# FFN down with twelve folded pairs and weight sums made ahead, in place of eight pairs with sums made on the spot

## The chip, the core and the metric

The kernel runs on one core of one Trainium2 chip. Its time is device microseconds. The profiled times below come from one execution of the kernel before; the time of the runs is the median of three.

## The reference

One layer over 256 latent tokens of width 2048, with 256 context tokens that only feed the attention. All is float32. Cut to what the change touches:

```python
mod = jax.nn.silu(c) @ w_mod[l] + b_mod[l]          # 6 * 2048 columns
...
y = (sigmoid(ga) * (oa @ w_br_a) + sigmoid(gb) * (ob @ w_br_b)) @ w_o
x = x + gt1 * rms_norm(y, g_attn_post[l])
h = modulate(rms_norm(x, g_ffn_pre[l]), sh2, sc2)
# conv_ffn: w_up is 2048 x 11264, w_down is 5632 x 2048
u = depthwise_conv(h @ w_up, conv_w, conv_b)        # three taps along the tokens
a, g = jnp.split(u, 2, axis=-1)
x = x + gt2 * rms_norm((silu(g) * a) @ w_down, g_ffn_post[l])
```

## The kernel before

**Products.** TensorE makes a float32 product out of three: both operands are split into a high part `hi` of type fp32r and a rest `lo`, and hi x hi, lo x hi and hi x lo are summed in PSUM (`product`, L1377). `split` (L140) makes the two parts of a tile: ACT copies the source into `hi` with rounding (L144), then DVE subtracts `hi` from the source (L148). So ACT's half always comes before DVE's half of the same tile, and a matmul can begin when the first is there.

**Weights.** `ws` holds the weights from the value projection to FFN down as blocks of 128 x 2048 floats (1 MB), in the order of use. `raw_block` (L130) loads one from SP's queue into a ring of four buffers (`raw`), which the tiles of the modulation (`wm_b`) go through too. `block` (L205) hands out the next block: it splits the one after it (`split_to`) and issues loads up to `ahead` blocks further (`load_to`); `halves` (L151) makes the `wh` and `wl` of a plain block in two halves of 1024 columns, in two sets of buffers. A raw buffer is free for its next load when both parts are made, or, for a modulation tile, when its product is done. SP issues its loads in the order of its list, so a load that waits for a buffer holds up those behind it.

**Modulation.** 64 of the columns of `mod` are made by DVE, one per tile of `wm_b`: `mods` (L237) multiplies the tile with the row of silu(c) (`crb`) and sums along it (L247, 128 x 2048). Six of them go beside Wo and sixteen beside FFN up.

**Wo.** `norm_gain` (from L981) multiplies by `w_o` in four chunks `c` of 512 output columns, each of four blocks `g`; a block is four contraction tiles times two token halves times three products, 24 matmuls at L994. Beside each block, `beside(c, g)` runs: the two loads of `x`, and in the first three chunks one modulation product behind each of the blocks g = 1, 2, 3. Six tiles are left by then, so the last calls do nothing.

**FFN up.** A loop over the 44 tiles `j` of the hidden width, each with an activation block (i = 0) and a gate block (i = 1). The work on the last block's result is queued behind the split of the next weights: evacuation (ACT `half_u` L222, DVE `u` L223), the convolution's taps (ACT L1264, DVE L1265 and L1267), and `gate` (L1271: silu, product and the split of the activations). In every even `j` from 4, behind the gate block, one modulation product runs on DVE.

**FFN down.** The hidden width is 44 contraction tiles; the output is made in two halves `h` of 1024 columns, as two chunks of 512. A **direct** block D (L1383) has four contraction tiles and one chunk: 4 tiles x 2 token halves x 3 = 24 matmuls. A **folded** block S (`fold`, L1390) has one pair of contraction tiles and both chunks: it takes the 2 x 2 blocks of the activations (two token halves, two tiles) and of the weights (two tiles, two chunks), forms sums of them, and makes seven products in place of eight, 7 x 3 = 21 matmuls, by Strassen's scheme. Three products use weights as they are (`wh`, `wl`), four use sums of weights (`th`, `tl`). `folded` (L181) makes both on the spot: two splits of the plain weights (512 and 1024 wide), four additions of 512 columns in place in the raw buffer (L190), two splits of the sums (1024 wide). The sums of the activations are made in `gate` (L1291) and kept split in `fs`, seven tiles per pair. `J0, NS` say that tiles 24 to 39 are the eight pairs; `SEQ` gives the order of blocks in a half:

```python
SEQ = "DSDSDSDDSDSDDSDSDSDDDD"   # 14 D, 8 S
wts = first_wts if h == n == 0 else block(3)
```

The products' sums are put together by closures (`late`) behind the half's last S.

**What sets the order.** The program is written in one order, and a scheduler makes a list per engine from it; `issue_after` holds a piece of work behind a given instruction. The engines run their lists in order and wait on each other by semaphores; a tile's next use waits for the readers of its buffer. POOL has no work in the stages that are touched.

## Time and profile before

| | us |
|---|---|
| median of 3 runs (1495.61 to 1495.78) | 1495.72 |
| the profiled execution | 1495.41 |
| its span | 1493.6 |
| PE busy in it | 1484.2 |
| DVE busy | 1220.0 |
| ACT busy | 821.9 |
| Wo, products at L994 | 672.95 to 760 |
| FFN up | to 1256.5 |
| FFN down, products at L1379 | 1256.7 to 1485.75 |

A row of a group reads: line, engine, operation, output <- inputs, shape and type of the output <- of the input, count, then busy time and the mean ns of one, then the idle time of the engine just before them and what ended it ("<-ACT wh L144": ACT's work on `wh`). A row of the timeline or chain starts with the time from the start of the span and the duration in us, and ends in the wait before it. A row of the windows has the stretch, its length, the busy us (and instructions) of PE, PEld, DVE, ACT and POOL, the granted clock of TensorE, the busy share of the DMA engines and GB/s. A row of the DMA issues ends in the median us from issue to landing. Shares above 1.00 come from packets that overlap in the records.

### The profile page before, as it was taken

How to read it: one execution, taken by the hardware profiler on the slowest of the kernel's cores; microseconds unless marked ns; L12 is line 12 of the kernel's file. 1: busy time of each engine (PE TensorE's matmuls, PEld its weight loads, DVE VectorE, ACT ScalarE, POOL GpSimd, SP SyncE). 2: the span in 40 equal slices, each digit the busy share in tenths (PEclk: the TensorE clock that was granted, in tenths of full speed). 3: DMA queues.
4: the chain of work that ended last, by engine and by line, in shares of the span. 5: the costliest groups of instructions: out<-in, count | busy, mean ns of one | idle time of the engine just before them, and what ended most of it. 6: DMA issues, size and time to landing. Idle time of an engine off the chain costs nothing.

```text
span 1493.6 us, 21738 instructions
## 1 busy us (share of the span) xinstructions
PE 1484.2 (99%) x8491; PEld 1279.4 (86%) x8491; DVE 1220.0 (82%) x1851; ACT 821.9 (55%) x1363; POOL 1.8 (0%) x11
## 2 busy tenths in 40 slices
PE   9999999999999999999999999999999999999998
PEld 6877889998888888888888888888888888888886
DVE  4499878989988888877877887887888878887887
ACT  5553324777764455455667555555555565455443
POOL 0000000000000000000000000000000000000000
PEclk9999999999999999999999999999999999999999
DMA  9988699754467888779856666766666654655652
GB/s 371 399 317 338 250 384 348 267 190 170 143 254 294 326 319 325 292 273 357 309 207 224 247 236 224 254 232 222 251 230 232 216 196 163 231 212 185 268 216 106
DMA packets 61159, 383.72 MB, mean 257 GB/s; under 512 B 6512, under 2 KB 8960, under 8 KB 18304
## 3 DMA queue, kind: packets, MB, share of 16 engines
q1 hardware_dynamic: 60480, 381.52, 68.3%
q8 instruction: 67, 1.10, 0.3%
q10 hardware_dynamic: 576, 0.80, 0.2%
q14 instruction: 36, 0.29, 0.1%
HBM read 378.05 MB, written 4.25 MB: 256 GB/s over the span
## 4 chain that ended last, share of the span: by engine, by line
PE 97%; DMA 1%; DVE 1%; ACT 1%; issue 0%; SPq 0%; DVEq 0%
PE pu L217 21%; PE c L1379 12%; PE pu L218 11%; PE pv L760 7%; PE pg L217 7%; PE pk L498 7%; PE py_o L994 6%; PE pq L217 4%; PE pb L217 4%; PE pg L218 4%; PE x L1379 3%; PE pq L218 2%; PE pb L218 2%; PE po L902 1%; PE s L871 1%; PE pt L893 1%
## 5 line engine op out<-in xcount | busy, mean ns | idle before, releaser
L148 DVE TENSOR_TENSOR wl<-raw,wh 128x1024 fp32r<-128x1024 f32 (+1 forms) x444 | 520.8, 1201 | 119.8 <-ACT wh L144 119.0
L144 ACT ACTIVATE wh<-raw 128x1024 fp32r<-128x1024 f32 (+1 forms) x444 | 444.7, 1037 | 204.9 <-PE pg L217 54.6
L217 PE MATMUL pu<-h,wh 128*128 128x512 f32 x1404 | 487.6, 390 | 0.0
L218 PE MATMUL pu<-h,wl 128*128 128x256 f32 x1404 | 395.9, 282 | 0.0
L217 PEld LDWEIGHTS pu<-h,wh 128*128 128x128 f32 x1404 | 263.6, 188 | 55.0
L218 PEld LDWEIGHTS pu<-h,wl 128*128 128x128 f32 x1404 | 265.4, 189 | 0.0
L217 PE MATMUL pg<-h,wh 128*128 128x512 f32 x464 | 161.5, 390 | 0.0
L1379 PE MATMUL c<-wh,ff 128*128 128x512 f32 x448 | 137.9, 389 | 0.0
L218 PE MATMUL pg<-h,wl 128*128 128x256 f32 x464 | 130.8, 282 | 0.0
L247 DVE SCALAR_TENSOR_TENSOR raw<-raw,crb 128x2048 f32<-128x2048 f32 x48 | 109.7, 2285 | 11.2 <-DMA raw<-in_wm_b_dram 11.1
L498 PE MATMUL pk<-h,ku 128*128 128x512 f32 x480 | 117.4, 398 | 0.8 <-ACT h L410 0.4
L222 ACT ACTIVATE half_u<-pu 128x256 f32<-128x256 f32 x88 | 33.4, 382 | 147.8 <-PE pu L218 147.8
L217 PE MATMUL pq<-h,wh 128*128 128x512 f32 x304 | 108.8, 396 | 0.1
L498 PEld LDWEIGHTS pk<-h,ku 128*128 128x128 f32 x480 | 87.7, 188 | 24.1 <-issue 3.9
L217 PEld LDWEIGHTS pg<-h,wh 128*128 128x128 f32 x464 | 87.1, 188 | 18.2
L760 PE MATMUL pv<-wh,h 128*128 128x512 f32 (+1 forms) x384 | 101.5, 354 | 0.0
L1379 PEld LDWEIGHTS c<-wh,ff 128*128 128x128 f32 x448 | 84.0, 188 | 17.3
L217 PE MATMUL pb<-h,wh 128*128 128x512 f32 x256 | 89.4, 390 | 0.0
L218 PEld LDWEIGHTS pg<-h,wl 128*128 128x128 f32 x464 | 87.7, 189 | 0.0
L1379 PE MATMUL c<-wl,ff 128*128 128x512 f32 x224 | 87.4, 390 | 0.0
L218 PE MATMUL pq<-h,wl 128*128 128x256 f32 x304 | 85.5, 281 | 0.0
L994 PE MATMUL py_o<-wh,zz 128*128 128x512 f32 x256 | 78.3, 389 | 0.0
(258 smaller groups left out, 2091.4 us busy)
## 6 DMA issues: line engine op xcount, KB each, us to landing
raw<-in_ws_dram SPq DMA_DIRECT2D x222, 1024.0 KB, 4.9
raw<-in_wm_b_dram SPq DMA_DIRECT2D x64, 1024.0 KB, 4.9
raw<-in_wm_sc_dram SPq DMA_DIRECT2D x15, 1024.0 KB, 7.6
raw<-in_wkt_dram SPq DMA_DIRECT2D x10, 1024.0 KB, 7.7
raw<-in_wm_sh_dram SPq DMA_DIRECT2D x8, 1024.0 KB, 9.5
sd<-in_wm_sd_dram SPq DMA_DIRECT2D x6, 1024.0 KB, 6.3
raw<-in_wk_dram SPq DMA_DIRECT2D x7, 768.0 KB, 8.1
crb<-sild SPq DMA_DIRECT2D x5, 1024.0 KB, 8.9
```

Source lines behind the costliest of these rows:

```text
L144: a_ = nc.scalar.activation(hi, src, AF.Copy)
L148: v_ = nc.vector.tensor_tensor(out=lo, in0=src, in1=hi, op=ALU.subtract)
L217: nc.tensor.matmul(pt[:, :], wh[:, w], a, start=first and i == 0, stop=False, skip_group_check=True)
L218: nc.tensor.matmul(pt[:, :S], wl[:, w], a[:, 0], start=False, stop=last and i == n - 1, skip_group_check=True)
L222: a_ = nc.scalar.activation(t[:], pt[:, S:], AF.Copy)
L247: nc.vector.scalar_tensor_tensor(out=r, in0=r, scalar=1.0, in1=row, op0=ALU.mult, op1=ALU.mult, accum_out=modx[:, j : j + 1])
L498: nc.tensor.matmul(pk[:], wt[:, w], hh[:, :, k, a], start=k == 0 and a == 0 and wt is wh, stop=k == KT - 1 and a == 1)
L760: nc.tensor.matmul(pv[i][:, :nw], src[:, k, a, t0 : t0 + P], wt[:, w], start=k == 0 and q == 0, stop=k == KT - 1 and q == 2)
L871: nc.tensor.matmul(s_ps, qs[hd][:, a, qt * P : qt * P + P], k_[:, w], start=q == 0, stop=q == 2)
L893: nc.tensor.transpose(pt[:, b * P : b * P + P], sms[hd, qt][:, b * P : b * P + P], ident[:])
L994: p_ = nc.tensor.matmul(py[t][:], act[:, k, a, t * P : t * P + P], wt[:, w], start=k == 0 and q == 0, stop=k == nk - 1 and q == 2)
L1379: nc.tensor.matmul(pt[:], a(i), wt[:, w], start=k not in begun, stop=stop and q == 2, skip_group_check=True)
```

## The change

**More pairs.** Tiles 16 to 39 are twelve pairs; a half of FFN down is 10 D and 12 S, in the order DSS, six times, and four D.

**Sums of weights ahead.** There are 24 blocks S (twelve pairs in two halves), and each needs one block of sums of weights (1 MB). They are made before FFN down and kept in DRAM (`sumd`): SP loads the S block into the raw ring (`load_sum`), DVE makes the sums in place in one subtraction of 1024 columns and two operations of 512 (`sum_part`), and POOL's queue writes the 1 MB to `sumd` (`nc.gpsimd.dma_start`). Four are made beside Wo: at block i = 4c + g of Wo stands a product of the modulation (m) or a sum (T) by `WO = " mmTmTmTmTm"`. Twenty are made beside FFN up, in the even j from 4; its modulation products go to the odd j from 5. In FFN down an S block loads its `sumd` (1 MB) and the three chunks of 512 columns of the plain weights (0.75 MB). The four additions in place are gone there.

**The order inside S.** The columns of an S block in `ws` stand in the order b1, a1, a0, b0. The four products of sums come first, in two tiles `t0` and `t1` with one buffer each, and the three of plain weights after them; the splits of the next S block's sums are put between the products.

**Four pairs unsplit.** Of pairs 2, 4, 6 and 8 the activations are kept as they are (`late_a`) and are summed and split in FFN down (`late_split`), in each half, in the D block ahead of the pair, into one buffer `late_f`.

```diff
@@ -56,9 +56,13 @@
-J0, NS = 24, 8
+J0, NS = 16, 12
 ND0 = (FT - 2 * NS) // 4
-SEQ = "DSDSDSDDSDSDDSDSDSDDDD"
+SEQ = "DSSDSSDSSDSSDSSDSSDDDD"
+LATE = (2, 4, 6, 8)
+NSUM = 2 * NS
+WO = " mmTmTmTmTm"
+SUMS_UP = range(4, FT, 2)
@@ -67,6 +71,15 @@
+def kept(p):
+    return p - sum(q < p for q in LATE)
+def block_of_sum(n):
+    h, p = divmod(n, NS)
+    return B_DN + h * len(SEQ) + [i for i, kind in enumerate(SEQ) if kind == "S"][p]
@@ -171,26 +185,57 @@
+    sum_of = {b0 + block_of_sum(n): n for n in range(NSUM)}
+    wsum, folding = {}, []
     def load_to(i):
         for q in range(min(i, len(srcs) - 1) + 1):
             if q not in raws:
-                raws[q] = raw_block(*srcs[q])
-
-    def folded(r):
...
+                if q in sum_of:
+                    wsum[q] = raw_block(sumd[sum_of[q]])
+                    nraw[0] += 1
+                    r = raws[q] = wp.tile([P, 2048], F32, tag="raw", bufs=4, name=f"raw{nraw[0]}")
+                    for w in (slice(0, 512), slice(1024, 2048)):
+                        sync.dma_start(out=r[:, w], in_=srcs[q][0][:, w])
+                else:
+                    raws[q] = raw_block(*srcs[q])
+    def split_sum(q, half):
+        w = slice(half * 1024, half * 1024 + 1024)
+        t = [folding[0].tile([P, 1024], F32R, tag=f"t{half}{c}", bufs=1, name=f"t{half}{c}{q}") for c in "hl"]
+        split(t[0][:], t[1][:], wsum[q][:, w])
+        parts[q][1].append(t)
+    def folded(q):
         h, lo = (
-            wp.tile([P, 2048 + 128], F32R, tag=f"w{q}", bufs=2, name=f"w{q}{nraw[0]}")[:, :2048] for q in "hl")
+            wp.tile([P, 2048 + 128], F32R, tag=f"w{c}", bufs=2, name=f"w{c}{q}")[:, :2048] for c in "hl")
+        parts[q] = (h, lo), []
+        if SEQ[(q - b0 - B_DN - 1) % len(SEQ)] == "D":
+            with tc.issue_after(last[0]), tc.issue_after(last[1]):
+                for half in range(2):
+                    split_sum(q, half)
+        for w in (slice(0, 512), slice(1024, 2048)):
+            split(h[:, w], lo[:, w], raws[q][:, w])
+    tosum, nsum = [], [0]
+    def load_sum():
+        if nsum[0] + len(tosum) < NSUM:
+            tosum.append(raw_block(ws[block_of_sum(nsum[0] + len(tosum))]))
+    def sum_part(i):
+        if not tosum:
+            return
+        r = tosum[0]
+        q = [r[:, n * 512 : n * 512 + 512] for n in range(4)]
+        if i == 0:
+            nc.vector.tensor_tensor(out=r[:, :1024], in0=r[:, :1024], in1=r[:, 512:1536], op=ALU.subtract)
+            return
+        nc.vector.tensor_tensor(out=q[2], in0=q[0], in1=q[2], op=ALU.add)
+        nc.vector.tensor_tensor(out=q[3], in0=q[3], in1=q[2], op=ALU.subtract)
+        nc.gpsimd.dma_start(out=sumd[nsum[0]], in_=tosum.pop(0))
+        nsum[0] += 1
@@ -1049,8 +1094,16 @@
-            if c < 3 and g:
-                mods(1, crb[:], (c, g) != (2, 3))
+            i = 4 * c + g
+            if i < len(WO):
+                with tc.issue_after(last[1]):
+                    if WO[i] == "T":
+                        sum_part(0)
+                        sum_part(1)
+                    elif i:
+                        mods(1, crb[:], 0)
+                if 0 < i < len(WO) - 1:
+                    (load_sum if WO[i + 1] == "T" else load_mod)()
@@ -1249,7 +1302,9 @@
-    fs = fp.tile([P, NS, 2, 7, P], F32R, name="fs")
+    fs = fp.tile([P, NS - len(LATE), 2, 7, P], F32R, name="fs")
+    late_a = fp.tile([P, len(LATE), 2, S], F32, name="late_a")
+    late_f = fp.tile([P, 2, 7, P], F32R, name="late_f")
@@ -1270,27 +1325,35 @@
-        nc.vector.tensor_tensor(out=a[:], in0=a[:], in1=g[:], op=ALU.mult)
+        p, odd = divmod(j - J0, 2)
+        o = late_a[:, LATE.index(p), odd] if is_folded(j) and p in LATE else a[:]
+        nc.vector.tensor_tensor(out=o, in0=a[:], in1=g[:], op=ALU.mult)
         if not is_folded(j):
             d = direct_tile(j)
             split(ff[:, d, 0], ff[:, d, 1], a[:])
...
+        elif p not in LATE:
+            if odd:
+                act_sums(bank(f"st{p}"), first[0][:], a[:])
+            act_split(fs[:, kept(p)], a[:], odd)
+            if odd:
+                act_split(fs[:, kept(p)], None, 2)
             first[:] = [a]
+    def act_split(dst, a, part):
+        hi, lo = (dst[:, q].rearrange("p i t -> p (i t)") for q in range(2))
+        o, w = ((0, P), (P, 2 * P), (3 * P, 4 * P))[part]
+        split(hi[:, o : o + w], lo[:, o : o + w], total[0] if part == 2 else a[:, :w])
+    def act_sums(t, e, a):
+        e0, e1 = e[:, :P], e[:, P:]
         t_ = [t[:, i * P : i * P + P] for i in range(4)]
         for o, x, y, op in (
+            (t_[2], e0, e1, ALU.subtract), (t_[0], e1, a[:, P:], ALU.add), (t_[1], t_[0], e0, ALU.subtract),
             (t_[3], a[:, :P], t_[1], ALU.subtract)):
             nc.vector.tensor_tensor(out=o, in0=x, in1=y, op=op)
-        split(hi[:, 3 * P :], lo[:, 3 * P :], t[:])
+        total[:] = [t[:]]
+    total = []
@@ -1318,7 +1381,12 @@
-                mods(i if j % 2 == 0 and j > 3 else 0, crb)
+                if j in SUMS_UP:
+                    sum_part(i)
+                elif i and j > 4:
+                    mods(1, crb, 0)
+                if i:
+                    (load_sum if j + 1 in SUMS_UP else load_mod if j > 3 else list)()
@@ -1387,18 +1455,30 @@
-        def fold(wts, p):
-            (wh, wl), (th, tl) = wts
+        def fold(wts, p, behind=None):
+            (wh, wl), (ta, tb) = wts
             sl = [slice(i * 512, i * 512 + 512) for i in range(4)]
-            A = lambda n: lambda i: fs[:, p, i, n]
+            f_ = late_f if p in LATE else fs[:, kept(p)]
+            A = lambda n: lambda i: f_[:, i, n]
             end = p == NS - 1
-            product(X[1], A(0), wh, wl, sl[1], 1, end)
+            product(X[7], A(5), *ta, sl[0], 7, end)
+            product(X[5], A(3), *ta, sl[1], 5, end)
+            if behind:
+                split_sum(behind, 0)
+            product(X[6], A(4), *tb, sl[0], 6, end)
+            product(C[1, 0], A(2), *tb, sl[1], (1, 0))
+            if behind:
+                split_sum(behind, 1)
+            product(X[1], A(0), wh, wl, sl[2], 1, end)
             product(C[0, 0], A(1), wh, wl, sl[3], (0, 0))
-            product(C[0, 1], A(6), wh, wl, sl[2], (0, 1))
-            product(X[5], A(3), th, tl, sl[0], 5, end)
-            product(X[6], A(4), th, tl, sl[1], 6, end)
-            product(X[7], A(5), th, tl, sl[2], 7, end)
-            product(C[1, 0], A(2), th, tl, sl[3], (1, 0))
+            product(C[0, 1], A(6), wh, wl, sl[0], (0, 1))
+        def late_split(p):
+            e, o = (late_a[:, LATE.index(p), q] for q in range(2))
+            with tc.issue_after(last[0]), tc.issue_after(last[1]):
+                act_sums(yp.tile([P, 512], F32, tag="asum", bufs=1, name=f"asum{h}_{p}"), e, o)
+                for part, a in ((2, None), (1, o), (0, e)):
+                    act_split(late_f, a, part)
@@ -1429,11 +1509,16 @@
-            wts = first_wts if h == n == 0 else block(3)
+            q = nblk[0] - (h == n == 0)
+            nxt = q + 1 if SEQ[(n + 1) % len(SEQ)] == "S" else None
+            wts = first_wts if h == n == 0 else block(2 if kind == "S" else 3)
+            if kind == "D" and nxt and f in LATE:
+                late_split(f)
             if late:
                 late.pop(0)()
             if kind == "S":
-                fold(wts, f)
+                fold(wts, f, nxt)
+                load_to(q + 3)
@@ -1588,7 +1673,7 @@
-                ws[B_DN + h * len(SEQ) + i] = np.concatenate([a[:, 1], a[:, 0], b[:, 1], b[:, 0]], axis=1)
+                ws[B_DN + h * len(SEQ) + i] = np.concatenate([b[:, 1], a[:, 1], a[:, 0], b[:, 0]], axis=1)
```

The lists show three places where instructions stand differently. The first is SP's list in Wo: `wm_b` are modulation tiles, `ws` weights, and with the change also S blocks to be summed (raw_6603, raw_6688, raw_6761). Before:

```order
L137 DMA raw_6543<-in_wm_b_dram 128x2048 [waits DMAHW5_49,DVE_49]
L137 DMA raw_6552<-in_ws_dram 128x2048 [waits DVE_49]
L137 DMA raw_6578<-in_wm_b_dram 128x2048 [waits DMAHW6_49,DVE_49]
L137 DMA raw_6587<-in_ws_dram 128x2048 [waits DMAHW7_49,DVE_49]
L137 DMA raw_6613<-in_wm_b_dram 128x2048 [waits DMAHW0_49,DVE_49]
L137 DMA raw_6634<-in_ws_dram 128x2048 [waits DMAHW5_49,DMAHW1_49,DVE_49]
L137 DMA raw_6666<-in_ws_dram 128x2048 [waits DMAHW2_49,DVE_49]
L137 DMA raw_6692<-in_wm_b_dram 128x2048 [waits DMAHW7_49,DMAHW3_49,DVE_49]
L137 DMA raw_6701<-in_ws_dram 128x2048 [waits DMAHW4_49,DVE_49]
```

And with the change:

```order
L151 DMA raw_6568<-in_wm_b_dram 128x2048 [waits DMAHW5_49,DVE_49]
L151 DMA raw_6576<-in_ws_dram 128x2048 [waits DVE_49]
L151 DMA raw_6603<-in_ws_dram 128x2048 [waits DMAHW6_49,DVE_49]
L151 DMA raw_6611<-in_ws_dram 128x2048 [waits DMAHW7_49,DVE_49]
L151 DMA raw_6641<-in_wm_b_dram 128x2048 [waits DMAHW0_49,DVE_49]
L151 DMA raw_6661<-in_ws_dram 128x2048 [waits DMAHW5_49,DMAHW1_49,DVE_49]
L151 DMA raw_6688<-in_ws_dram 128x2048 [waits DMAHW7_49,DMAHW2_49,DVE_49]
L151 DMA raw_6696<-in_ws_dram 128x2048 [waits DMAHW6_49,DMAHW3_49,DMASW0_49]
L151 DMA raw_6726<-in_wm_b_dram 128x2048 [waits DMAHW4_49,DVE_49]
```

Between two modulation tiles there now stand a block to be summed and two weight blocks, where one weight block or two stood. The weights W8 (raw_6696) wait for DMASW0, which is POOL's write of the first sum (raw_6603), since they go into its buffer; before, every load waited for DVE or for another load alone.

The second place is DVE in FFN up, around a gate block of an even `j` and the block behind it. Before:

```order
L223 TENSOR_TENSOR u_8090<-pu_0_8057,half_u_8091 128x256
L148 TENSOR_TENSOR wl_8095<-raw_7998,wh_8094 128x1024 x2
L1273 TENSOR_TENSOR a_8004<-a_8004,a_8053 128x256
L1265 SCALAR_TENSOR_TENSOR a_8106<-u_8090,col,a_8106 128x255
L247 SCALAR_TENSOR_TENSOR raw_7903,modx<-raw_7903,ff 128x2048
L148 TENSOR_TENSOR ff<-a_8004,ff 128x256
L1267 SCALAR_TENSOR_TENSOR a_8106<-u_8090,col,a_8106 128x255
L223 TENSOR_TENSOR u_8146<-pu_1_8113,half_u_8147 128x256
```

With the change (L268 is the `u` of the block, L162 a split, L233, L235 and L236 the sum, L1320, L1322 and L1330 the taps and the gate):

```order
L268 TENSOR_TENSOR u_8316<-pu_1_8283,half_u_8317 128x256
L162 TENSOR_TENSOR wl_8321<-raw_8221,wh_8320 128x1024 x2
L1320 SCALAR_TENSOR_TENSOR a_8328<-u_8316,col,a_8328 128x255
L233 TENSOR_TENSOR raw_8281<-raw_8281 128x1024
L1322 SCALAR_TENSOR_TENSOR a_8328<-u_8316,col,a_8328 128x255
L268 TENSOR_TENSOR u_8366<-pu_0_8333,half_u_8367 128x256
L162 TENSOR_TENSOR wl_8371<-raw_8270,wh_8370 128x1024 x2
L1330 TENSOR_TENSOR a_8276<-a_8276,a_8328 128x256
L1320 SCALAR_TENSOR_TENSOR a_8382<-u_8366,col,a_8382 128x255
L235 TENSOR_TENSOR raw_8281<-raw_8281 128x512
L162 TENSOR_TENSOR ff<-a_8276,ff 128x256
L236 TENSOR_TENSOR raw_8281<-raw_8281 128x512
```

The sum is spread over two blocks, 1024 columns behind the split of the one and twice 512 behind that of the next; the wide product of L247 that stood behind a split has moved to the odd `j`.

The third place is ACT at the seam from FFN up to FFN down. Before, wh_11837 and th_11839 are the first S (plain weights and sums), wh_11890 is the second D, and wh_11919 and th_11921 the second S:

```order
L144 ACTIVATE wh_11890<-raw_11774 128x1024
L144 ACTIVATE ff<-a_11780 128x256
L144 ACTIVATE wh_11890<-raw_11774 128x1024
L144 ACTIVATE wh_11919<-raw_11853 128x512
L144 ACTIVATE wh_11919<-raw_11853 128x1024
L144 ACTIVATE th_11839<-raw_11720 128x1024 x2
L144 ACTIVATE th_11921<-raw_11853 128x1024 x2
```

With the change, wh_11997, t0h_11999 and t1h_12003 are the first S, and wh_12048, t0h_12060 and t1h_12070 the second, which follows at once:

```order
L158 ACTIVATE wh_11997<-raw_11876 128x1024
L1319 ACTIVATE a_11981<-u_11977,col 128x256
L1327 ACTIVATE a_11981<-a_11981 128x256
L158 ACTIVATE ff<-a_11940 128x256
L158 ACTIVATE wh_12048<-raw_11933 128x512
L158 ACTIVATE t0h_11999<-raw_11874 128x1024
L158 ACTIVATE t1h_12003<-raw_11874 128x1024
L158 ACTIVATE wh_12048<-raw_11933 128x1024
L158 ACTIVATE t0h_12060<-raw_11931 128x1024
L158 ACTIVATE t1h_12070<-raw_11931 128x1024
```

The first S's sums are split between the two pieces of the second S's plain weights, and so behind the 512-wide one; before, they stood behind all of the second S's plain weights.

More of the change, by code (lines that the diff above doesn't have):

```diff
@@ L125, in layer_kernel @@
     shd = tc.dram_tile([3, D], F32, name="shd")
+    sumd = [tc.dram_tile([P, 2048], F32, name=f"sumd{n}") for n in range(NSUM)]
     nraw = [0]
@@ L176, in load_to @@
             if q not in raws:
-                raws[q] = raw_block(*srcs[q])
-    folding = []
-    def folded(r):
-        sl = [slice(i * 512, i * 512 + 512) for i in range(4)]
-        h, lo = (
-            wp.tile([P, 2048 + 128], F32R, tag=f"w{q}", bufs=2, name=f"w{q}{nraw[0]}")[:, :2048] for q in "hl")
-        th, tl = (folding[0].tile([P, 2048], F32R, tag=f"t{q}", bufs=1, name=f"t{q}{nraw[0]}") for q in "hl")
-        for q in (sl[1], slice(1024, 2048)):
-            split(h[:, q], lo[:, q], r[:, q])
-        for o, a, b, op in ((2, 2, 0, ALU.subtract), (0, 0, 1, ALU.subtract), (1, 2, 1, ALU.add), (3, 3, 1, ALU.subtract)):
-            nc.vector.tensor_tensor(out=r[:, sl[o]], in0=r[:, sl[a]], in1=r[:, sl[b]], op=op)
-        for q in (slice(0, 1024), slice(1024, 2048)):
-            split(th[:, q], tl[:, q], r[:, q])
-        return (h, lo), (th, tl)
+                if q in sum_of:
[6 more added lines that the diff above has]
+                    raws[q] = raw_block(*srcs[q])
@@ L200, in split_to @@
                 if d >= 0 and SEQ[d % len(SEQ)] == "S":
-                    parts[q] = folded(raws[q])
+                    folded(q)
                 else:
```

10 lines of the change are left out of this document (removed).

## The prediction

> **What bounds the kernel now.** I read the page's busy times and chain first, then busy time by stage, then the chain in order of time.
>
> ```profile
> span 1493.6 us, 21738 instructions
> PE 1484.2 (99%) x8491; PEld 1279.4 (86%) x8491; DVE 1220.0 (82%) x1851; ACT 821.9 (55%) x1363; POOL 1.8 (0%) x11
> PE 97%; DMA 1%; DVE 1%; ACT 1%; issue 0%; SPq 0%; DVEq 0%
> ...
> 672.95 87.07 PE py_o L994 x384
> ...
> 1256.70 5.45 PE c L1379 x24
> ...
> 1463.28 22.45 PE c L1379 x99
> ```
>
> TensorE carries the chain and hardly pauses. So a matmul removed is worth its whole time, and anything else costs only what makes TensorE wait. The last row gives the price of a 512-column product: 22.45/99 = 0.2268 us. Stages differ in what else is near its limit:
>
> ```profile
> 695.00:700.00 5.00, 5.00 (x23) 4.13 (x22) 4.39 (x6) 4.38 (x10) 0.00 (x0) 1.00 1.02 431
> 700.00:705.00 5.00, 5.00 (x24) 4.14 (x23) 4.53 (x5) 1.97 (x3) 0.00 (x0) 1.00 0.88 279
> 710.00:715.00 5.00, 5.00 (x24) 4.14 (x23) 4.69 (x5) 3.80 (x6) 0.00 (x0) 1.00 1.07 426
> 1000.00:1100.00 100.00, 100.00 (x579) 88.63 (x578) 83.87 (x129) 57.63 (x93) 0.00 (x0) 1.00 0.67 241
> 1300.00:1350.00 50.00, 50.00 (x222) 41.41 (x221) 43.65 (x47) 27.81 (x32) 0.00 (x0) 1.00 0.53 203
> ```
>
> Columns: length, then PE, PEld, DVE, ACT, POOL, granted clock, DMA share, GB/s. In Wo (the first three) the DMA engines are full; in FFN up and down (the last two) they have a third or more to spare, and DVE is the busy one.
>
> **The gain.** A pair of contraction tiles, in one half of the output, is 2 tiles x 2 token halves x 2 chunks x 3 = 24 matmuls direct and 7 x 3 = 21 folded. Four more pairs in two halves save 24 matmuls: 24 x 0.2268 = 5.44 us. That is all there is to win.
>
> **Wo: four sums go where the DMA is full.** Block n of the sixteen starts at 672.95 + 5.44 n (87.07/16). What its neighbours wait for:
>
> ```profile
> 698.12 2.01 ACT L144 ACTIVATE wh<-raw 128x1024 fp32r<-128x1024 f32 x2 [0.38 <-DMA raw<-in_ws_dram]
> 703.17 2.01 ACT L144 ACTIVATE wh<-raw 128x1024 fp32r<-128x1024 f32 x2 [3.03 <-DMA raw<-in_ws_dram]
> 709.09 2.01 ACT L144 ACTIVATE wh<-raw 128x1024 fp32r<-128x1024 f32 x2 [3.91 <-DMA raw<-in_ws_dram]
> ...
> 710.18 4.85 DVE L148 TENSOR_TENSOR wl<-raw,wh 128x1024 fp32r<-128x1024 f32 x4 [1.35 <-ACT wh L144]
> ...
> crb<-sild SPq DMA_DIRECT2D x1, 1024.0 KB, 6.1
> ...
> raw<-in_ws_dram SPq DMA_DIRECT2D x1, 1024.0 KB, 7.4
> ...
> raw<-in_ws_dram SPq DMA_DIRECT2D x1, 1024.0 KB, 7.7
> ...
> raw<-in_ws_dram SPq DMA_DIRECT2D x2, 1024.0 KB, 4.8
> ```
>
> Block 7 starts at 711.0 and its weights landed at 709.09; its first low half is made from 710.18 to about 711.4, and its third matmul wants it at 711.5. The stage has no slack left, although nothing stalls. The last four rows are single transfers: the first of the stage's train (issued 678.44, landed 684.5), two issued at 701.6 and 703.8 (landed 709.0 and 711.5, so 2.45 us apart: the price of 1 MB in a full queue) and, as the last, two in FFN up (issued between 1006 and 1012), where the queue is short.
>
> The change keeps the six modulation products here, spread to later blocks, and adds four reads and four writes of 1 MB. By bandwidth alone: up to the weights of block 11 the lists of SP and POOL hold 21 transfers (the row of silu(c), the gain row, two of x, four modulation tiles, seven weight blocks W5 to W11, three raw pairs read, three sums written), and from the first landing 684.5 + 20 x 2.45 = 733.5. Block 11 starts at 672.95 + 59.8 = 732.8 and needs its high half (1.05 us) first, so 731.7: at least 1.8 us of stall. That is the lower end. The upper end gives each write half of the DMA while it lasts: the sum of the first pair ends near 704.0 (its DVE work, 2.5 us, fits in behind the split that ends at 701.5), the write starts about 705.3 and pushes W7 from 709.0 to 711.3; block 7 then starts 1.7 us late. Its successors: W8 sits in the buffer that this write must free, and behind its landing DVE has the second sum (2.5 us) and the two closing products of the chunk to do before W8's low half: 0.6 us more. Reckoned in the same way (a buffer is free when its sum is written or its product done, 1 MB lands some 7 us after that, a sum stands ahead of the split on DVE), blocks 9 to 13 come 0.2, 0.75, 1.1, 0.8 and 0.5 us later still. Sum 5.7 us. Either way the stall appears as TensorE idle in Wo. I take the middle, 3.75 us, as the DMA is full in most of the stage but falls to 279 GB/s after 700, where a write may slip in.
>
> The Trainium skill, page "DMA: Bandwidth & Descriptors", section "SWDGE vs HWDGE vs iDMA", says that transfers issued from GpSimd and those issued from SP feed different queues inside a DMA engine, which takes turns between them. By that rule the upper end would hold and the sum below would be 2.0 us worse. No run here shows a transfer from POOL.
>
> **FFN up: twenty sums.** One period of four blocks on DVE:
>
> ```profile
> 1018.54 0.42 DVE L223 TENSOR_TENSOR u<-pu,half_u 128x256 f32<-128x256 f32 x1 [1.32 <-ACT half_u L222]
> 1019.49 2.36 DVE L148 TENSOR_TENSOR wl<-raw,wh 128x1024 fp32r<-128x1024 f32 x2 [0.52 <-ACT wh L144]
> ...
> 1022.50 2.29 DVE L247 SCALAR_TENSOR_TENSOR raw<-raw,ff 128x2048 f32<-128x2048 f32 x1
> ...
> 1025.44 0.42 DVE L223 TENSOR_TENSOR u<-pu,half_u 128x256 f32<-128x256 f32 x1
> ...
> 1029.63 0.42 DVE L223 TENSOR_TENSOR u<-pu,half_u 128x256 f32<-128x256 f32 x1 [0.59 <-ACT half_u L222]
> 1030.58 2.36 DVE L148 TENSOR_TENSOR wl<-raw,wh 128x1024 fp32r<-128x1024 f32 x2 [0.52 <-ACT wh L144]
> ...
> 1035.18 0.42 DVE L223 TENSOR_TENSOR u<-pu,half_u 128x256 f32<-128x256 f32 x1 [0.65 <-ACT half_u L222]
> 1036.13 2.36 DVE L148 TENSOR_TENSOR wl<-raw,wh 128x1024 fp32r<-128x1024 f32 x2 [0.52 <-ACT wh L144]
> 1040.72 0.42 DVE L223 TENSOR_TENSOR u<-pu,half_u 128x256 f32<-128x256 f32 x1 [1.32 <-ACT half_u L222]
> ```
>
> From 1018.54 to 1040.72 are 22.2 us, four blocks of 5.55. Idle in them, with the last row's 1.32 in place of the first's, and 0.52 in front of the split that follows it: 0.59 + 0.52 + 0.65 + 0.52 + 1.32 + 0.52 = 4.1 us. Prices for what is added:
>
> ```profile
> L148 DVE TENSOR_TENSOR wl<-raw,wh 128x1024 fp32r<-128x1024 f32 x114 | 135.3, 1221 | 20.7 <-ACT wh L144 20.7
> L190 DVE TENSOR_TENSOR raw<-raw 128x512 f32<-128x512 f32 x32 | 22.1, 692 | 1.0
> L148 DVE TENSOR_TENSOR fs<-st,fs 128x512 fp32r<-128x512 f32 x8 | 5.5, 683 | 0.0
> L1291 DVE TENSOR_TENSOR st<-a 128x128 f32<-128x128 f32 x8 | 2.3, 293 | 0.0
> L144 ACT ACTIVATE th<-raw 128x1024 fp32r<-128x1024 f32 x16 | 16.1, 1052 | 29.0 <-DVE raw L190 29.0
> L144 ACT ACTIVATE wh<-raw 128x512 fp32r<-128x512 f32 x9 | 5.6, 623 | 11.9 <-PE c L1379 10.4 <-PE pu L217 0.9 <-ACT x L1414 0.7
> ```
>
> One sum per period is one 1024-wide and two 512-wide subtractions, 1.22 + 2 x 0.69 = 2.6 us. It leaves 1.5 us of idle; the folded pairs whose activations are split at once add about 1.8 (four of 0.29, one of 0.68) and use that up, for one period each, before a period without. DVE then falls behind by at most some 2.4 us, and TensorE needs the next split (first half done 2.7 us into a block of 5.55) 2.9 us later plus the 0.5 us of wait that vanishes. I charge 0.2 us. The modulation products also move to odd blocks; each still stands behind a split, and only the two short convolution steps and the evacuation queue behind it. A sum holds its buffer until it is written: ended 1.3 blocks after it began, some 6 us for the write, 5 for the next load, so the weights of four blocks later arrive more than half a block early. Nothing hides this but that slack.
>
> **FFN down: the start.** Products of sums now come first, and the order puts the 512-wide split of the second pair's weights ahead of the first pair's sums on ACT. That split waits for the buffer of the first direct block.
>
> ```profile
> 1257.42 1.05 ACT L144 ACTIVATE wh<-raw 128x1024 fp32r<-128x1024 f32 x1
> ...
> 1261.99 0.61 PE L1379 MATMUL x<-wh,fs 128*128 128x512 f32 x2
> ```
>
> The first direct block ends at 1262.0; ACT then does 0.62 + 1.05 us and TensorE has three matmuls (0.68) that don't need it: a stall of about 0.8 us. Before, the products of plain weights stood first and covered this.
>
> **FFN down: the period D S S.** It lasts 24 + 21 + 21 matmuls, 14.96 us. DVE splits 2 x 1024 + 2 x (512 + 3 x 1024): 8 of 1.22 and 2 of 0.69, 11.1 us, and with an unsplit pair four sums of 0.29 and splits of 0.29, 0.42 and 0.68, another 2.6. The four additions in place that each folded block had (4 x 0.69) are gone. 13.7 of 14.96 fits, but the last split of an unsplit pair, after two that wait for ACT, ends within 0.2 us of its first use. Eight such pairs: 0 to 2.5 us, I take 0.6, near the low end since consecutive ops overlap (two of 1.22 take 2.36). SP loads 4.5 MB per period, 11 us at 2.45: it fits.
>
> **The sum.** -5.44 + 3.75 + 0.2 + 0.8 + 0.6 = -0.1 us against the profiled execution, whose own time is 1495.41, 1.8 above its span; the median of the runs is 1495.72, 0.3 above that. Forecast 1495.6: the matmuls go, and the waits give their time back.
>
> **Rivals.**
> R1, the writes slip in. The DMA's 279 GB/s after 700 us speaks for it, the shares above 1.00 around it against. Then Wo costs at most 1.0 and the rest 1.0: 1495.7 - 5.4 + 2.0 = 1492.3, and 1490.5 with no stall at all.
> R2, slower: in FFN up the pair to be summed lands late, and DVE, which works in order, waits for it. A load alone takes 4.8 us, and by the chain of buffers the sum finds it about 1.0 us after landing. DMA there rises from 241 GB/s by 2 MB per 22.2 us to some 335. If loads then take 7.4 as in Wo, DVE waits 1.6 us per period; where a period has no idle left (the eight with folded activations) TensorE loses 1.3 to 1.6 us each, 10 to 13 in all: about 1506; half the delay about 1500. It decides from a landing of 5.9 us on. Against it: 335 is far below 426.
> R3, slower at Wo: the writes that POOL issues start late, each by one DVE instruction (1.2 us, the row of L148 above), because POOL's work on them stands back while DVE works. Four of them add up to 4.8 us to the stall in Wo: 1495.6 + 4.8 = 1500.4; it decides once a write starts 0.8 us late (3.0/4). No row of the trace of before has such a write, for or against it. The Trainium skill, page "SBUF — State Buffer", section "Summary: rules for kernel authors", advises against GpSimd-issued transfers beside busy DVE, because their descriptors can't be written during DVE's two-port modes; its section "Who interferes with whom" says that tensor_tensor has no such mode, which speaks against the full price here; no run here shows either.
>
> **The numbers.** A measurement of this kernel tells 0.2%, 3.0 us, from no change. No change (1492.7 to 1498.7): 0.43. R1, the part of it below 1492.7: 0.32. R2: 0.15. Wo at its upper end and beyond, with R3: 0.10. The forecast's own range is 1492.9 (Wo 1.0) to 1498.6 (Wo 5.7 and the unsplit pairs at 1.6). The range for 8 in 10 takes in most of R1 and half of R2: 1490.6 to 1500.5.
>
> **What would show it.** TensorE idle between blocks 7 and 13 of Wo, ended by ACT's or DVE's split behind a DMA: 2 to 6 us, else R1. One gap of about 0.8 us just after the first direct block of FFN down. FFN up without idle on TensorE, DVE at 93 to 95% there; idle of TensorE with DVE waiting for a raw pair's DMA would be R2. 24 matmuls fewer in FFN down, and its length 223 to 225 us instead of 229. Wrong would be the whole account if TensorE idled in FFN down by more than 3 us.

## The result: 8.5 us slower, and all of it in Wo

| | before | changed |
|---|---|---|
| median, us | 1495.66 (1495.49 to 1495.78, 4 runs) | 1504.14 (1503.02 to 1504.88, 4 runs) |
| ratio to before | 1 | 1.0056, 95% interval 1.0039 to 1.0074 |
| span of the profiled execution | 1493.6 | 1501.2 |
| Wo, first product to the first matmul behind it | 87.05 | 98.86 |
| FFN up, from there to the first product of FFN down | 496.7 | 496.7 |
| FFN down, first to last direct product | 228.6 | 224.6 |

The forecast was 1495.6, in a range of 1490.6 to 1500.5. The gain came nearly as reckoned, FFN up cost nothing, and Wo cost three times the 3.75 us put down for it. The profiled execution is the shortest of the four (1503.02): its span is 7.6 us longer than before, 11.8 in Wo less 4.0 in FFN down and some 0.2 elsewhere. The page of the changed kernel (busy times, then the chain by engine):

```profile
span 1501.2 us, 22074 instructions
PE 1485.5 (99%) x8467; PEld 1276.1 (85%) x8467; DVE 1256.2 (84%) x1923; ACT 842.0 (56%) x1395; POOL 14.7 (1%) x35
PE 91%; DMA 4%; DVE 2%; ACT 1%; issue 0%; SPq 0%; ACTq 0%; DVEq 0%
```

24 matmuls fewer (8491 before), and yet TensorE is busy 1.3 us longer: busy time that grows while the work shrinks means a slower matmul. In the chain the share of TensorE fell from 97% to 91%; transfers and splits now end last for a while. Two rows say where the stages lie: the first matmul after Wo, of before and of the changed kernel.

```profile
759.84 1.02 PE L1114 MATMUL pu<-x,ident 128*128 128x512 f32 x2
```

```profile
771.80 1.02 PE L1167 MATMUL pu<-x,ident 128*128 128x512 f32 x2
```

What TensorE waited for in the changed kernel (the view of waits: engine, line, what for; us in total, times, longest):

```profile
PE py_o L1039 <- ACT wh L158: 4.4, 3, 2.1
...
PE py_o L1039 <- DVE wl L162: 1.1, 2, 0.6
PE x L1447 <- ACT t0h L158: 0.8, 1, 0.8
```

5.5 us of gaps stand at Wo (L1039), two of them 2.08 and 2.03 us long; before, Wo had none. What these two cost does not end with them. The timeline of TensorE, and the windows around it (the third number from the end is the granted clock):

```profile
718.92 1.86 PE L1039 MATMUL py_o<-wh,zz 128*128 128x512 f32 x4 [2.08 <-ACT wh L158]
...
734.42 1.21 PE L1039 MATMUL py_o<-wh,zz 128*128 128x512 f32 x4 [2.03 <-ACT wh L158]
```

```profile
718.50:719.00 0.50, 0.08 (x1) 0.08 (x1) 0.38 (x3) 0.50 (x2) 0.00 (x0) 1.00 1.04 442
719.00:719.50 0.50, 0.50 (x2) 0.42 (x3) 0.50 (x1) 0.50 (x1) 0.00 (x0) 0.69 1.04 442
722.00:722.50 0.50, 0.50 (x3) 0.41 (x2) 0.50 (x1) 0.00 (x0) 0.00 (x0) 0.50 0.88 262
722.50:723.00 0.50, 0.50 (x3) 0.40 (x3) 0.50 (x1) 0.00 (x0) 0.00 (x0) 0.90 0.77 279
...
736.00:736.50 0.50, 0.50 (x3) 0.43 (x2) 0.50 (x1) 0.00 (x0) 0.00 (x0) 0.76 0.90 246
739.50:740.00 0.50, 0.50 (x3) 0.36 (x3) 0.00 (x0) 0.00 (x0) 0.00 (x0) 0.83 1.06 442
```

After the gap that ends at 718.92 the clock is at 0.50 from 719.2 to 722.6, and after the one that ends at 734.42 from 736.3 to 739.6: 3.4 us each at half speed, 1.7 us lost each. So of the 11.8 us (98.86 - 87.05), 5.5 are gaps and 3.4 are half clock. The other 2.9 have no row of their own; part of them are short waits at the start of a block that are drawn as longer matmuls.

Why the weights were late stands in the chain of waits in order of time (start, us, what):

```profile
717.45 0.30 issue
717.75 10.74 DMA sumd<-raw
728.49 0.02 issue
728.51 4.72 DMA raw<-in_ws_dram
...
733.32 1.06 ACT wh L158
```

The write of the second sum starts 0.3 us after DVE made it and takes 10.74 us in the full DMA. The next weights go into its buffer, so SP can issue their load only at 728.51; they land at 733.23, ACT splits them from 733.32, and TensorE, which was done with the block before at 732.4, starts at 734.42. All loads behind that one in SP's list stand too. The first gap follows the first write (issued at 705.10, landed 7.8 us later) in the same way.

FFN up in the changed kernel has no gap: TensorE is busy throughout the window, with DVE at 90% and the DMA at 321 GB/s.

```profile
1000.00:1260.00 260.00, 260.00 (x1502) 230.49 (x1501) 235.31 (x367) 146.26 (x234) 6.39 (x12) 1.00 0.86 321
```

### The profile page after: what moved, and what is told of

It reads as the page before. It is cut to its first block, busy times and chain, and to the rows that moved or that the text cites. A ratio compares the mean times of both kernels' runs of the same rounds, so it can differ in the third digit from the quotient of the medians.

```text
span 1501.2 us, 22074 instructions
## 1 busy us (share of the span) xinstructions
PE 1485.5 (99%) x8467; PEld 1276.1 (85%) x8467; DVE 1256.2 (84%) x1923; ACT 842.0 (56%) x1395; POOL 14.7 (1%) x35
## 4 chain that ended last, share of the span: by engine, by line
PE 91%; DMA 4%; DVE 2%; ACT 1%; issue 0%; SPq 0%; ACTq 0%; DVEq 0%
PE pu L262 21%; PE pu L263 11%; PE c L1447 10%; PE pv L805 7%; PE pg L262 7%; PE pk L543 7%; PE pq L262 4%; PE x L1447 4%; PE pb L262 4%; PE pg L263 4%; DMA raw<-in_ws_dram 3%; PE pq L263 2%; PE py_o L1039 2%; PE pb L263 2%; PE po L947 1%; PE s L916 1%
## 5 line engine op out<-in xcount | busy, mean ns | idle before, releaser
L162 DVE TENSOR_TENSOR wl<-raw,wh 128x1024 fp32r<-128x1024 f32 (+1 forms) x444 | 518.1, 1191 | 118.0 <-ACT wh L158 117.0
L1447 PE MATMUL c<-wh,ff 128*128 128x512 f32 x320 | 98.5, 389 | 0.0
L1039 PE MATMUL py_o<-wh,zz 128*128 128x512 f32 x256 | 80.4, 402 | 4.4 <-ACT wh L158 4.4
L805 PEld LDWEIGHTS pv<-wh,h 128*128 128x128 f32 x384 | 67.7, 189 | 10.1
L263 PE MATMUL pb<-h,wl 128*128 128x256 f32 x256 | 72.2, 282 | 0.0
```

The source lines that it names most:

```text
L162: v_ = nc.vector.tensor_tensor(out=lo, in0=src, in1=hi, op=ALU.subtract)
L263: nc.tensor.matmul(pt[:, :S], wl[:, w], a[:, 0], start=False, stop=last and i == n - 1, skip_group_check=True)
L805: nc.tensor.matmul(pv[i][:, :nw], src[:, k, a, t0 : t0 + P], wt[:, w], start=k == 0 and q == 0, stop=k == KT - 1 and q == 2)
L1039: p_ = nc.tensor.matmul(py[t][:], act[:, k, a, t * P : t * P + P], wt[:, w], start=k == 0 and q == 0, stop=k == nk - 1 and q == 2)
L1447: nc.tensor.matmul(pt[:], a(i), wt[:, w], start=k not in begun, stop=stop and q == 2, skip_group_check=True)
```

## The experiments

Three questions: is the loss Wo alone; is it the write that holds the buffer, the bandwidth, or DVE; and what does a gap do to the clock. Behind each time stand its ratio to the kernel before and the 95% interval of the ratio; where two runs of one kernel are all there is, the time alone.

**All sums beside FFN up.** Wo gets its modulation products back, and the four sums go to the free odd j at the end.

```diff
-WO = " mmTmTmTmTm"
-SUMS_UP = range(4, FT, 2)
+SUMS_UP = (*range(4, FT, 2), 37, 39, 41, 43)
...
```

> The changed kernel with Wo as it was before (modulation products alone) and all 24 sums beside FFN up (the four that stood in Wo go to the odd j 37, 39, 41 and 43, where no modulation product is left). Theory A, the whole loss is in Wo: the 12.0 us that Wo became longer are gone, 1504.1 - 12.0 = 1492.1, no idle in Wo, FFN down as in the change (225.3 us). Rival B, FFN up has no room for more sums: TensorE idles between j = 37 and 43 by 1 us or more per sum, 1496 or more.

1503.45 us (1.005, 1.0036 to 1.0064). Wo is 87.06 us long, as before, so its 11.8 us are gone. But a new gap stands at the seam to FFN down:

The waits, then the chain, then a window of it:

```profile
PE x L1438 <- ACT t0h L157: 6.8, 1, 6.8
...
PE pu L262 <- DVE wl L161: 1.3, 2, 0.8
```

```profile
1249.90 7.98 DMA sumd<-raw
...
1258.28 5.11 DMA raw<-in_ws_dram
...
1265.76 5.64 DMA raw<-in_ws_dram
...
1272.02 1.05 ACT t0h L157
```

```profile
1260.00:1280.00 20.00, 12.53 (x45) 9.36 (x44) 13.34 (x20) 10.17 (x14) 0.53 (x1) 0.83 0.87 298
```

It is the same mechanism at another place: the write of the last sum but one holds the buffer that FFN down's first S block needs, its load begins 8 us after the sum is made, the load behind it (for the second S, which ACT splits ahead of `t0h`) later still, and the gap of 6.8 us brings the mean granted clock of its 20 us to 0.83 (the window). Theory A was right on Wo and wrong on the time; rival B's place was right, and its reason (no room in FFN up) was not the main one, as the later runs show.

**Sums without writes.** The four sums of Wo are made and dropped.

```diff
...
-        nc.gpsimd.dma_start(out=sumd[nsum[0]], in_=tosum.pop(0))
+        if nsum[0] > 3:
+            nc.gpsimd.dma_start(out=sumd[nsum[0]], in_=tosum[0])
+        tosum.pop(0)
```

> The changed kernel, but the first four sums are made in Wo and not written (FFN down takes the plain block in their place, of the same size; that part of the result is left out). Theory A1, the write holds the buffer that the next weights need: without it a buffer is free when DVE is done, idle of TensorE in Wo falls from 5.5 us to under 1, the granted clock stays at 1.00, about 1493. Rival A2, the DMA is simply full: half of the added 8 MB are still there, idle falls to about half, 2 to 3 us, and the time is 1497 to 1500.

1495.73 us (0.9999, 0.9989 to 1.0009). Wo takes 91.23 us, gaps 2.0 us in all, none above 0.9, granted clock 1.00 throughout. Its waits:

```profile
PE py_o L1041 <- DVE wl L162: 1.1, 3, 0.6
PE py_o L1041 <- ACT wh L158: 0.9, 1, 0.9
```

**Sums in buffers of their own.** Reads, sums and writes stay; only the ring of four is left to the weights and the modulation.

```diff
...
+            if own:
+                r = own[0].tile([P, 1984], F32, tag="own", bufs=2, name=f"own{nsum[0]}")
+                sync.dma_start(out=r[:], in_=src[:, :1984])
+                tosum.append(r[:])
...
```

> The changed kernel, but the blocks to be summed in Wo go to two buffers of their own and not through the ring of four (1984 of their 2048 columns, for space; FFN down takes the plain block in place of the first four sums; that part of the result is left out). Reads, sums and writes stay. Theory A1, a weight block waits for the write because it needs that buffer: idle in Wo falls to 1 to 2 us (what bandwidth alone costs), no drop of the clock, 1493 to 1495. Rival A2, the full DMA is the cause: idle and time stay, 1500 to 1504.

1496.26 us (1.0006, 0.9996 to 1.0016). Wo takes 91.09 us. Both runs agree: of Wo's 11.8 us, 7.6 to 7.8 go (the two drops of the clock among them) when the weights no longer wait for a write, and about 4 stay whether the write is there or not. So A1 carries two thirds; both times lie above its range and below that of A2. Each run takes away something else too: the first the 4 MB of the writes, the second the places of the summed blocks in the ring. That both give the same speaks for the wait, but no run takes away the wait alone.

**No work on DVE.** As the run before, but what is read is written back unchanged.

```diff
...
+        if own and i == 0:
+            return
...
```

> As the run with own buffers beside Wo, but DVE makes no sums there: what is read is written back as it is (that part of the result is left out). Reads and writes stay at 8 MB. Theory D, the 4.5 us that Wo is still longer with own buffers come from DVE's sums (2.6 us each, ahead of the splits): Wo is at most 1.8 us longer than before, 1492 to 1493.5. Rival: it is the bandwidth of the added transfers, Wo stays 4 us or more longer, 1495 to 1496.

1498.09 us (1.0014, 1.0004 to 1.0024); Wo takes 94.02 us, 3 more than with the sums, and the time lies above both ranges. Theory D falls: without DVE's work the loss is no smaller. Without the sums the writes begin when the read has landed (at 701.5, 713.8, 726.7 and 738.8, against 705.1, 714.2, 729.3 and 739.9), and the weights land later (the DMA issues from 672 to 765):

```profile
raw<-in_ws_dram SPq DMA_DIRECT2D x17, 1024.0 KB, 11.1
```

With the sums the median was 9.2 us, in the kernel before 6.8. TensorE waits mostly for ACT's splits, and those for the transfers:

```profile
PE py_o L1048 <- ACT wh L158: 3.3, 4, 0.9
```

So the full queue is the likely price of the rest: 4 us with the writes later, 7 with the writes earlier. It is not shown apart from the sums, since leaving them out also moved the writes; what DVE's time alone costs stays open.

**Gaps put into the kernel before.** Three, then six, chains of copies on ACT that TensorE waits for in Wo, nothing else changed. The first:

```diff
...
+                nc.scalar.activation(st[:], py[1][:, :S], AF.Copy)
+                for _ in range((2, 4, 6)[c] - 1):
+                    nc.scalar.activation(st[:], st[:], AF.Copy)
+                stalled[:] = [nc.tensor.transpose(bank(f"stall{c}")[:, :P], st[:, :P], ident[:]).ins]
```

> The kernel before with three stalls of TensorE put into Wo, behind chunks 0, 1 and 2: ACT copies the finished product 2, 4 and 6 times in a chain and TensorE waits for it, some 1.0, 1.7 and 2.4 us. Nothing else is late there. Theory C, a gap of about 2 us brings the granted clock to 0.50 for 3.4 us: the time grows by the gaps (5.1 us) and by 1.7 us for each gap that does it, one or two of them, 1502.5 to 1504.2. Rival, a gap costs its own length: 1500.8, clock 1.00 throughout.

1508.46 us. ACT had other work in between, so the gaps were 1.39, 2.25 and 5.45 us:

```profile
696.51 0.33 PE L1023 MATMUL stall<-ident,st 128*128 128x128 f32 x1 [1.39 <-ACT st L1022]
...
720.87 0.33 PE L1023 MATMUL stall<-ident,st 128*128 128x128 f32 x1 [2.25 <-ACT st L1022]
...
748.46 0.47 PE L1023 MATMUL stall<-ident,st 128*128 128x128 f32 x1 [5.45 <-ACT st L1022]
```

The clock stayed at 1.00 behind the first two, and fell to 0.50 for 6.8 us (746.6 to 753.5) in the third. So 2.25 us did not drop it, while 2.03 and 2.08 in the changed kernel did: length alone doesn't decide. The second, with chains of seven copies behind every second block:

> The kernel before with six equal gaps of TensorE in Wo, about 2 us each, behind every second block of the first three chunks (a chain of seven copies on ACT that TensorE waits for). Theory C1, a gap of 2 us drops the clock according to where it falls: some of the six are followed by 3.4 us at 0.50 and some by none, and the time grows by the gaps (12 us) and 1.7 us for each that is. Rival C2, the length alone decides: all six or none, 22 us or 12 us in all.

1540.89 us; the gaps were 3.8 to 6.5 us, not 2, and all six were followed by half clock, so it could not tell C1 from C2. But the slow stretches begin at 687.8, 704.9, 725.4, 745.8, 762.9 and 780.0, each 5 or 6 times 3.41 us after the one before. The third, with four copies:

> As the run with six gaps, whose gaps came out at 3.8 to 6.5 us and were all followed by half clock, but with chains of four copies in place of seven: gaps of about 2.2 us, longer where ACT has other work. Theory C1, the clock is set on a grid of 3.41 us by how much TensorE idled in the period that ends: gaps near 2 us that lie within one period are followed by 3.4 us at 0.50, those that a border cuts in two are not. Rival C2, the length decides: none below a fixed length and all above it, wherever they lie.

1518.76 us. The ends of the six gaps, and the windows at the first and the fifth:

```profile
687.29 0.48 PE L1026 MATMUL mark<-ident,st 128*128 128x128 f32 x1 [2.84 <-ACT st L1025]
...
702.55 0.33 PE L1026 MATMUL mark<-ident,st 128*128 128x128 f32 x1 [2.33 <-ACT st L1025]
...
715.30 0.33 PE L1026 MATMUL mark<-ident,st 128*128 128x128 f32 x1 [1.39 <-ACT st L1025]
...
730.03 0.33 PE L1026 MATMUL mark<-ident,st 128*128 128x128 f32 x1 [3.36 <-ACT st L1025]
...
744.20 0.33 PE L1026 MATMUL mark<-ident,st 128*128 128x128 f32 x1 [2.79 <-ACT st L1025]
...
760.54 0.33 PE L1026 MATMUL mark<-ident,st 128*128 128x128 f32 x1 [3.39 <-ACT st L1025]
```

```profile
687.00:687.50 0.50, 0.21 (x2) 0.21 (x2) 0.50 (x1) 0.24 (x1) 0.00 (x0) 0.74 1.13 475
690.50:691.00 0.50, 0.50 (x3) 0.40 (x2) 0.00 (x0) 0.00 (x0) 0.00 (x0) 0.84 0.89 377
...
730.00:730.50 0.50, 0.47 (x3) 0.43 (x4) 0.50 (x1) 0.50 (x1) 0.00 (x0) 1.00 0.99 344
...
745.00:745.50 0.50, 0.50 (x3) 0.41 (x3) 0.00 (x0) 0.00 (x0) 0.00 (x0) 0.77 0.00 0
748.50:749.00 0.50, 0.50 (x3) 0.37 (x3) 0.00 (x0) 0.00 (x0) 0.00 (x0) 0.82 0.29 115
...
760.50:761.00 0.50, 0.46 (x3) 0.42 (x4) 0.21 (x2) 0.50 (x3) 0.00 (x0) 1.00 1.04 426
```

The clock drops after 2.84 and 2.79 us and not after 3.36 and 3.39. The slow stretches begin at 687.24 and 745.27 (a mean of 0.74 in half a us at 1.00 and then 0.50 puts the edge 0.26 before its end), 17 periods of 3.41 us apart. On that grid the gaps of 2.84 and 2.79 put 2.8 and 2.3 us of idle into one period; the gaps of 3.36 and 3.39 are cut in two by a border (at 728.2 and 758.9), 1.8 us at most on a side, and so are the 2.33 (at 700.9) and, from the slow stretch at 746.6 back, the 2.25 of the first of these runs (at 719.3), which did not drop the clock either. In the changed kernel the slow stretches begin at 719.19 and 736.26, five periods apart. The first gap lies whole in the period ahead (2.08 us of 3.41); of the second 1.6 us do, with 0.5 us of short waits behind it (five matmuls from 734.42 to 736.02 take 1.60 us where 1.13 are due). C1 holds: from about 2 us of idle within one period, the next 3.41 us run at half clock. Two runs of the spread sums, below, bear it out where nothing was put in. The Trainium skill, page "TensorE: Matmul & The Clock Gate", section "Part 1: The HAM clock gate (the "warmup" mystery)", states such a free-running window of 3.4 us and two speeds; these runs agree on both. Its section "HAM oscillation — how this bites in real kernels" sums the rule up as no idle gaps above about 3.4 us, and there the runs differ: a gap of 2.03 us dropped the clock. That gaps of 3.36 and 3.39 did not fits both.

**FFN down alone.** No sums made ahead at all; FFN down loads plain blocks in their place.

```diff
...
-                    wsum[q] = raw_block(sumd[sum_of[q]])
+                    wsum[q] = raw_block(srcs[q][0])
...
```

> The changed kernel without any sums made ahead: Wo as before, the modulation products of FFN up at the odd j, no S block read or written there, and FFN down loads plain S blocks in place of the sums (the sums of weights are left out of the result). Theory: what is left is the gain of the folded pairs less the start of FFN down, FFN down 225.3 us as in the changed kernel or less, everything else as before: 1495.6 - 4 = 1491 to 1492. Rival: FFN down itself, with 4.5 MB per period and the unsplit pairs, loses what the matmuls win, 1494 or more.

1490.92 us (0.9969, 0.9958 to 0.998): FFN down with twelve pairs is worth 4.7 us of the possible 5.44 by the medians (in the profiled execution FFN down is 3.9 us shorter). The rest of the story is what the sums cost.

**The sums spread.** Wo as before; sums and modulation products evenly over j = 3 to 42.

```diff
+UP = dict(enumerate("TmTTm" * 7 + "mmTTT", 3))
...
+                if UP.get(j) == "T":
+                    sum_part(i)
+                elif i and UP.get(j) == "m":
+                    mods(1, crb, 0)
...
```

> Wo as before, all 24 sums beside FFN up, but spread evenly with the modulation products over j = 3 to 42 (sum, product, sum, sum, product seven times, then two products and three sums), so that the last sums no longer stand in a row of seven up to the seam. Theory A, the 6.8 us at the seam of the first try came from the crowded end (writes that hold the ring's buffers while FFN down's first loads wait): idle there is at most 1 us, Wo is 87 us, FFN down 225.3 us, and the time is 1491 to 1493. Rival B, FFN up has no room for 24 sums and 16 products wherever they stand: idle of several us in FFN up or at the seam, 1496 or more.

1494.65 us (0.9993, 0.9984 to 1.0001). The gap at the first S is 1.9 us in place of 6.8, so the crowded end was most of its cause; it isn't gone, and the time lies between the ranges of A and B. Next, with the first S's sums split ahead of the second S's plain weights:

```diff
...
+            split(h[:, w], lo[:, w], raws[q][:, w], held_by if q == b0 + B_DN + 2 else None)
...
```

> As the run with the even spread, and at the start of FFN down ACT splits the first pair's sums ahead of the second pair's plain weights (which wait for the first direct block's buffer). Theory: the one gap of 0.83 us at the first S is gone and the time is 0.8 us below the even spread alone. Rival: the gap moves to the second S, whose plain weights now come later, and the time is the same.

1493.94 us (0.9985, 0.9976 to 0.9994), 0.7 below, but the profiled execution still shows 2.4 us at the first S, since the plain weights of that S landed late and ACT's and DVE's work on the last tiles of FFN up stood behind them. The 0.7 lies within the spread of the runs of both (1492.5 to 1496.7 and 1491.95 to 1495.3), so it settles nothing.

The clock tells the two profiled executions apart. The gap and a window at its end, first of the even spread:

```profile
1264.95 2.00 PE L1438 MATMUL x<-t0h,fs 128*128 128x512 f32 x4 [1.91 <-ACT t0h L157]
```

```profile
1265.00:1265.50 0.50, 0.50 (x2) 0.41 (x3) 0.50 (x1) 0.50 (x1) 0.00 (x0) 0.56 0.76 287
```

Then of the new order:

```profile
1266.51 1.21 PE L1440 MATMUL x<-t0h,fs 128*128 128x512 f32 x4 [2.38 <-ACT t0h L157]
```

```profile
1266.50:1267.00 0.50, 0.49 (x2) 0.44 (x3) 0.50 (x1) 0.50 (x1) 0.00 (x0) 1.00 1.08 459
```

The gap of 1.91 us brought a period at half clock (1265.06 to 1268.48, 1.7 us lost), the longer one of 2.38 none. The grid says why. Its period is 3.4133 us (27 of them from 687.82 to 779.98 in the run with six long gaps), and the clock also falls on it when TensorE runs out of work at the end: in the even spread at 1490.34, 66 periods behind 1265.06. In the new order it falls at 1490.63; 66 periods ahead of that lies 1265.35, which cuts the gap (1264.13 to 1266.51) into 1.22 and 1.16. The gap of 1.91 (1263.04 to 1264.95) lies whole in the period that ends at 1265.06.

Then two j earlier, and the first S's sums ahead of its own plain weights too:

```diff
+UP = dict(enumerate("T" + "TmTTm" * 7 + "TmTm", 2))
...
+            split(h[:, w], lo[:, w], raws[q][:, w], last_t[:] if b0 + B_DN + 1 <= q <= b0 + B_DN + 2 else None)
...
```

> Wo as before, the 24 sums and 16 products spread over j = 2 to 41 so that the last sum is made at j = 40 and written some 25 us before FFN down begins; and at the start of FFN down the first two S blocks' sums are split ahead of their plain weights. Theory A (the idle at the seam in the even spread, 1.9 to 2.4 us, came from the last three writes and from splits that waited for late plain weights): TensorE idles at most 0.5 us between FFN up and the second S, FFN down takes 224 to 225 us, and the time is 1490 to 1492. Rival: the spread runs' FFN down was long for another reason, idle there stays near 2 us and the time near 1494.

1492.55 us (0.9982, 0.9974 to 0.9991); the gaps at the first and the third S are 0.5 and 0.7 us. That is 0.6 us above theory A's range, and FFN down takes 226.2 us (first to last direct product) where A said 224 to 225. In this run the product at j = 41 reads its row after it has been overwritten, so one column of the second gain is not right. Last, the products at j = 39 and 40 and the last sum at j = 41 ("TmmT" in place of "TmTm"):

> As the run with the early end, but with the last two modulation products at j = 39 and 40 and the last sum at j = 41, so that no product reads the row of silu(c) after the last activations have overwritten it (there the product at j = 41 did, and its column of the second gain was changed). Every output is computed. Theory A: like the early end, idle of at most 0.5 us at the first S, 1491.5 to 1493. Rival: one j later is late enough for the last write to hold up FFN down's loads again, 1494 as in the even spread.

1492.60 us (0.9981, 0.9972 to 0.999): 3.0 us faster than before and 11.5 faster than the change as it was made, with every output computed. Its waits:

```profile
PE x L1439 <- DVE late_f L161: 0.7, 1, 0.7
PE pu L262 <- DVE wl L161: 0.6, 1, 0.6
```

FFN up does have room for 24 sums and 16 products; 1.7 us (1492.6 - 1490.9) are between this run and the run without any sums. Its runs spread from 1491.5 to 1495.3, those of the kernel before in the same job from 1495.15 to 1496.39; what makes the spread wider wasn't settled (a gap near 2 us that costs 1.7 us more when it falls within one period could do it, which no run here shows).

## Why the prediction was wrong, point by point

**The gain** (-5.44): right. FFN down is 4.0 us shorter, and what it gives back was foreseen in size: the gap at the first S measured 0.83 us against 0.8, in the order named (the 512-wide split on ACT at 1273.90, then `t0h` at 1274.48). Whether that split waited for the first D's buffer, as the prediction has it, isn't shown: at the same moment ACT came free from the split of the last activations (`ff`, from 1273.58). The 0.6 for the unsplit pairs stands for one visible wait of 0.2 and some 0.4 without a row, whose cause isn't shown.

**Wo** (+3.75, at most 5.7): this term failed, at 11.8. The place, the releaser (a split behind a DMA) and the chain (the write frees a weight block's buffer late, first that of block 8, then that of block 10) were as described. Four sizes were off. The gaps came to 5.5 us, the upper end, where the middle was taken. The writes took 7.1 to 10.7 us, not the 6 to 7 taken from reads, and SP's list stood behind each. And the price of a gap was taken to be its length: two drops of the clock added 3.4 us that the trace of before, without a gap in Wo, could not show; the prediction named no case in which a stall costs more than itself. The last 2.9 us have no gap of their own and no term in the sum; part of them are the short waits at the start of the late blocks. In all 5.5 + 3.4 + 2.9 = 11.8. The lower end was wrong as well: against a floor by bandwidth of 1.8 us, Wo was 4 to 7 us longer with the ring out of the way.

**FFN up** (+0.2): right, 0 measured. DVE was busy 90%, below the 93 to 95 named.

**R1** (the writes slip in) fell with the first gap. **R2** (the pair lands late in FFN up) happened in small: DVE waits 5.2 us in 18 sums for the pair's transfer, 0.3 each, and TensorE never notices. Reads took 6.3 us there, beyond the 5.9 from which R2 was to decide, so that mark was set too low. The group on DVE from 840 to 1240 us in the changed kernel, then the DMA issues from 830 to 1240:

```profile
L233 DVE TENSOR_TENSOR raw<-raw 128x1024 f32<-128x1024 f32 x18 | 22.0, 1222 | 5.2 <-DMA raw<-in_ws_dram 5.2
```

```profile
sumd<-raw POOLq DMA_DIRECT2D x19, 1024.0 KB, 4.6
```

**R3** (POOL's writes start late) had the stage and the sign right and the mechanism wrong: each of the 24 writes was issued 0.3 to 0.6 us after the DVE instruction that it waits for, and the row above shows that beside a DVE at 90% the writes of FFN up land in 4.6 us, faster than the reads there (6.3). The writes of Wo, with DVE less busy (76.2 of 98.9 us), are the slow ones; there the DMA engines' share is 0.94 in the mean, against 0.86 in FFN up, so the full queue is the likely reason. For the Trainium skill's advice against such transfers (page "SBUF — State Buffer", section "Summary: rules for kernel authors") no run here shows a cost.

The range, 1490.6 to 1500.5, left 1504.1 outside because both ends of Wo's price were ends of a gap's length.

## What to carry to other kernels

A write back from a ring of load buffers isn't priced by its bytes: it lengthens the life of a buffer by its whole latency in the queue as it then is, and an in-order list of loads stands behind it; give such data buffers of its own, or put it where the next loads have slack, and not at a seam. When a chain that keeps TensorE at 99% gets a gap, price the gap by what the clock does afterwards, too. And a stage with no slack left is worth looking for in the profile before any work is moved into it: four sums cost 11.8 us beside Wo, and all 24 together less than 2 beside FFN up, once they were spread and ended early.

## What the runs showed of the hardware

- The granted clock is decided on a free-running grid of 3.41 us: about 1.9 us of idle within one period (1.83 did not, 1.91 did, by the records of TensorE) are followed by one period at 0.50, which costs 1.7 us; a gap of 3.39 us cut by a border cost only itself, and long gaps (3.8 us and more) cost one to three periods. In a slow period less idle is enough to stay slow: 0.9 us were in the run with six long gaps, 0.5 were not. These are the figures of Wo and FFN down: at the start of that same run, where many products are narrow (32 columns wide), a period with 1.2 us of idle was followed by a slow one (8.56 to 11.98 us).
- Writes of 1 MB from POOL's queue land in 4.6 us where the DMA engines' share is 0.86 in the mean and in 7.1 to 10.7 us where it is 0.94, and they start 0.3 us (0.6 in two of 24) after the DVE instruction that they wait for, with DVE 77% busy in Wo and 90% in FFN up.
